# Gate and q projections as seven block products instead of eight, over pairs of token blocks

## The chip, the cores and the metric

The kernel runs on one core of one Trainium2 chip. The metric is device time in microseconds, from one launch. The engines are named as the profile names them: PE (TensorE matmul), PEld (TensorE weight load), DVE (VectorE), ACT (ScalarE), POOL (GpSimd) and SP (SyncE, which here only issues DMAs). Each engine works through its own instruction queue in order and waits on semaphores for the others.

## The reference

One layer of a latent backbone with 2048 latent tokens, 256 context tokens and width 1024, all in float32:

```python
h_lat = _rmsnorm(x, norm_g[i]) * (1.0 + scale) + shift        # (2048, 1024)
h_ctx = _rmsnorm(ctx, norm_g[i]) * (1.0 + scale_c) + shift_c  # (256, 1024)
na_q, na_k, na_v, na_g, r_q, r_k, r_v, r_g = _split_proj(h_lat @ w_in)   # w_in: (1024, 4096)
o_na = _neighbourhood_attention(...)       # 8 heads of 64, 8 x 16 window and all context keys
y_na = _merge(o_na) * silu(na_g)
o_ret = o_f + flip(o_b)                    # 4 retention heads of 128, both directions
y_ret = _head_rmsnorm(o_ret, ret_norm_g) * silu(r_g)
x = x + gate * (concatenate([y_na, y_ret]) @ w_out)
return _rmsnorm(x, final_norm_g)
```

What matters here is the projection h @ w_in, above all the columns of na_q (0 to 511), na_g (1536 to 2047) and r_g (3584 to 4095), which only latent tokens need.

## The kernel before

Activations are kept transposed, 128 rows of the 1024 features to a partition tile (KC = 8 tiles along the feature axis), in four latent blocks of 512 tokens and one context block of 256. Every float32 operand of the projections is split into a rounded high part and the low rest, and a product is made of three matmuls (high x high, high x low, low x high); so each feature tile costs three matmuls. The block `blk[b]` is a pair of tiles, `hhi` and `hlo`, of 16 KB a partition each. Blocks 0 and 1 lie in the pool `hx` and blocks 2 and 3 in the pool `hy`, each with two buffers for each name.

Weights come in sets of 256 columns. `w_raw` loads one in two halves of 512 KB into the pool `st` (four buffers), `w_split` has ACT round the high part `whi` (L336) and POOL subtract it (`wlo`, L338), into the pool `wa` with two buffers of each. `load_w` issues the next set's load on SP's queue.

A unit of work is one of two forms. `tform` (L357) makes 128 columns for 512 tokens: 24 matmuls of 128x512. `tokform` (L368) makes 256 tokens by 256 columns: 48 matmuls of 128x256. Each takes one PSUM bank, of which the pool `pp` has six and the pool `psm` two. Both are generators with eight yields, so that they can be cut into pieces. The tile `o` that a unit's result is written to, on the way to DRAM, has two buffers. `store` puts off the issue of a DMA until the next `tick`; after the k projections the stores go out on ACT's queue.

The order of the work is the order of the program: nothing reorders it within an engine. In time, it is

- the k projections with the preparation of the blocks, by the list `PLAN`;
- `run_jobs`: v for all tokens (`u_v`, whose eviction is two casts on ACT, two subtractions on DVE and eight DMAs, four each on ACT's and SP's queues), four context units, then gates (`u_gate`, one SiLU on ACT) and q (`u_q`, a cast on ACT and a subtraction on DVE), eight units to a set of columns. Beside them `spill_step` writes blocks 2 and 3 to DRAM on SP's queue, and hooks behind the units of three sets prepare the output weights: `wo_gate` (L568, DVE adds one row block of the gate columns, eight times), `wo_row` (L575, four matmuls), `wo_mul` (L579, DVE multiplies a row block of `w_out`; ACT and POOL split it, L583 and L584; ACT stores it), eight times. All of these read one tile `wraw` with a single buffer, reloaded on SP's queue (L565) when the last reader is done;
- attention: 131 steps, in each of which pieces of the remaining projection units (the generator `fill_stream`, 48 units of eight pieces) stand between the matmuls of attention (L754, L781, L783, L802, L804). `quota` hands the pieces out evenly, with `held` = 66 kept for the stage behind. The four last q units come ahead of it, and blocks 2 and 3 are read back during it;
- retention with the output projection.

## Time and profile before

| | us |
|---|---|
| median of 3 runs | 1389.71 (1388.34 to 1392.48) |
| profiled execution, its own time | 1387.86 |
| its span, first to last instruction | 1386.1 |
| PE busy in the span | 1339.7 (97%) |
| DVE / ACT / POOL busy | 641.4 / 530.6 / 494.2 |
| granted TensorE clock, mean | 0.997 |
| v, context, gate and q units (from 166.6 to 561.7) | 395 |
| attention stage (562 to 1037) | 475 |

A line of the chain of waits gives the start, the length and what ran, with the count of instructions that follow each other; the length over the count is their spacing. A line of the instruction groups ends in the busy time and the mean duration of one in ns, and behind the next bar in the idle time of the engine before it and what ended it. A matmul's duration there includes its passage through the array, which overlaps the next one's; the spacing is read from the chain. A line of the order of time gives start, duration, engine, line, operation and in brackets the idle time before it with its releaser. A line of the table of stretches gives the stretch, its length, each engine's busy time with the count of its instructions, the granted clock, the DMA engines' busy share and GB/s.

### The profile page before, as it was taken

Reading aid. Unit: us, or ns where it says so; the run is one execution under the profiler, and the core shown is the slowest. Engines: PE = TensorE matmul, PEld = TensorE weight load, DVE = VectorE, ACT = ScalarE, POOL = GpSimd, SP = SyncE. Lnnn points to the kernel's source line nnn. Section 1 sums busy time; section 2 is a strip of 40 time slices with the busy share of each in tenths; the row PEclk is TensorE's granted clock in tenths of the full one; section 3 lists DMA queues with packets and bytes.
Section 4 is the critical chain, followed back from the end, with each engine's and each line's share of the span. In section 5 each row is a group of like instructions: output and inputs, shape, how many; then the busy total and the mean of one; then the engine's idle time right before and its main releaser. Section 6 shows DMA issues by size and latency. Waiting matters only on the chain.

```text
span 1386.1 us, 22777 instructions
## 1 busy us (share of the span) xinstructions
PE 1339.7 (97%) x8380; PEld 1172.7 (85%) x8380; DVE 641.4 (46%) x1244; ACT 530.6 (38%) x1155; POOL 494.2 (36%) x499
## 2 busy tenths in 40 slices
...
GB/s 315 173 162 125 184 253 279 228 130 106 47 166 131 220 256 258 207 169 208 188 174 211 203 223 267 267 209 161 196 84 261 257 286 287 175 168 168 160 115 129
DMA packets 218705, 270.45 MB, mean 195 GB/s; under 512 B 16865, under 2 KB 163425, under 8 KB 217570
## 3 DMA queue, kind: packets, MB, share of 16 engines
...
## 4 chain that ended last, share of the span: by engine, by line
PE 79%; DVE 7%; DMA 5%; issue 3%; POOL 3%; ACT 2%; SPq 1%; POOLq 0%; ACTq 0%; DVEq 0%
PE mm L357 26%; PE mm L368 19%; PE mm L1198 11%; PE sS L754 4%; PE tr L781 3%; PE po L802 3%; PE mm L921 2%; PE tr L783 2%; PE po L804 2%; PE mm L301 1%; PE mm L1110 1%; PE mm L1109 1%; PE mm L1108 1%; DMA v<-rvS 1%; PE mm L1089 1%
## 5 line engine op out<-in xcount | busy, mean ns | idle before, releaser
L357 PE MATMUL mm<-hhi,whi 128*128 128x512 f32 x640 | 259.0, 405 | 0.0
L357 PE MATMUL mm<-hlo,whi 128*128 128x512 f32 x640 | 253.1, 396 | 5.6 <-DVE hlo L270 2.2
L357 PE MATMUL mm<-hhi,wlo 128*128 128x512 f32 x640 | 252.9, 395 | 0.3 <-DVE wlo L338 0.3
L368 PE MATMUL mm<-whi,hhi 128*128 128x256 f32 x768 | 224.1, 292 | 0.0
L368 PE MATMUL mm<-wlo,hhi 128*128 128x256 f32 x768 | 216.7, 282 | 2.4 <-POOL wlo L338 2.4
L368 PE MATMUL mm<-whi,hlo 128*128 128x256 f32 x768 | 215.5, 281 | 0.0
L338 POOL TENSOR_TENSOR wlo<-st,whi 128x256 fp32r<-128x256 f32 (+1 forms) x97 | 112.3, 1175 | 243.1 <-ACT whi L336 240.6
L785 ACT CAST pt<-tr 128x640 fp32r<-128x640 f32 (+1 forms) x128 | 95.7, 748 | 191.7 <-PE tr L783 181.0
L791 DVE TENSOR_TENSOR pt<-tr,pt 128x640 fp32r<-128x640 f32 (+1 forms) x128 | 113.9, 890 | 91.3 <-ACT pt L785 90.6
L368 PEld LDWEIGHTS mm<-wlo,hhi 128*128 128x128 f32 x768 | 144.6, 188 | 3.1 <-POOL wlo L338 3.0
L357 PEld LDWEIGHTS mm<-hlo,whi 128*128 128x128 f32 x640 | 120.4, 188 | 31.3 <-issue 3.3
L357 PEld LDWEIGHTS mm<-hhi,wlo 128*128 128x128 f32 x640 | 120.1, 188 | 29.4 <-DVE wlo L338 0.7
L368 PEld LDWEIGHTS mm<-whi,hlo 128*128 128x128 f32 x768 | 144.9, 189 | 0.0
L368 PEld LDWEIGHTS mm<-whi,hhi 128*128 128x128 f32 x768 | 144.9, 189 | 0.0
L357 PEld LDWEIGHTS mm<-hhi,whi 128*128 128x128 f32 x640 | 120.3, 188 | 28.5 <-issue 4.6
L774 POOL TENSOR_SCALAR sp<-sp,stt 128x640 f32<-128x640 f32 (+2 forms) x128 | 103.7, 812 | 106.9 <-DVE stt L773 63.0
L763 DVE CUSTOM_DVE_ANT_0 sp<-sS,nb 128x640 f32<-128x640 f32 (+2 forms) x128 | 105.5, 825 | 22.4 <-PE sS L754 13.4
L768 ACT ACTIVATE sp<-sp,stt 128x640 f32<-128x640 f32 (+2 forms) x128 | 107.5, 840 | 15.4 <-DVE stt L763 15.0
L754 PE MATMUL sS<-k,q 128*128 128x256 f32 (+3 forms) x512 | 98.5, 314 | 4.4 <-DVE stt L763 3.4
L1198 PE MATMUL mm<-wor,y 128*128 128x512 f32 x384 | 95.6, 398 | 1.8 <-DVE xt L1207 1.2
L754 PEld LDWEIGHTS sS<-k,q 128*128 128x128 f32 x512 | 83.4, 188 | 11.2 <-DVE stt L763 5.5
L1198 PE MATMUL mm<-won,y 128*128 128x512 f32 x336 | 89.9, 406 | 0.0
...
## 6 DMA issues: line engine op xcount, KB each, us to landing
...
```

Source lines behind the costliest of these rows:

```text
L338: eng.tensor_tensor(l, r, f(h), ALU.subtract)
L357: nc.tensor.matmul(pm[:, :n], ww[:, k, cs], h[:, k, :], start=(k == 0 and i == 0), stop=(k == KC - 1 and i == 2))
L368: nc.tensor.matmul(pm[:, t * WG:(t + 1) * WG], h[:, k, o:o + P], ww[:, k, :], start=(k == 0 and i == 0), stop=(k == KC - 1 and i == 2))
L754: nc.tensor.matmul(o, hd["q"][i][:, hl, j * P:(j + 1) * P], k, start=(hl == 0), stop=(hl == 1))
L763: nc.vector.tensor_tensor_reduce(T["sp"][:, :n], T["s"], nbz[big][:, o:o + n], -1.0, 3e38, ALU.add, ALU.min, T["st"][:, 0:1])
L768: nc.scalar.activation(sp[:, :n], sp[:, :n], AF.Exp, bias=st[:, 0:1], scale=-1.0, accum_out=st[:, 1:2])
L774: nc.gpsimd.tensor_scalar(sp[:, :n], sp[:, :n], st[:, 2:3], 0.0, ALU.mult, ALU.add)
L781: nc.tensor.transpose(tr[:cn, g, :], sp[:, T["lo"] + g * cn:T["lo"] + (g + 1) * cn], ident)
L785: nc.scalar.copy(pt[:, :ng_ + 2, 0, :], tr[:, :ng_ + 2, :])
L791: nc.vector.tensor_tensor(pt[:, :n, 1, :], tr[:, :n, :], f(pt)[:, :n, 0, :], ALU.subtract)
L802: nc.tensor.matmul(po[:, t % 2, :, :], hd["vt"][kr0 // 4 + g][:cn, VORD.index(j), :], pt[:cn, g, :, :], start=(g == 0), stop=False)
L1198: nc.tensor.matmul(pm, yy[:, k, :], ww[:, k, sl], start=(k == 0 and i == 0), stop=(k == 3 and i == 2))
```

## The change

For each set of 256 columns (two column groups of 128) and each pair of token blocks A and B, the product is treated as a 2 by 2 product of blocks: feature halves on the inner side, the two column groups on one outer side and the two token blocks on the other. Eight block products become seven, with sums of weight blocks (`w_sums`) and of token blocks (`h_sums`) ahead and sums of products behind, in the form with 15 additions. `w_set` computes one set: seven `prod` of 12 matmuls each, with the sums of the products taken by DVE out of PSUM and the SiLU, or for q the scale of 0.125 and the split, afterwards (`fin`).

- The pair (0, 1) goes first. Its four token sums, high and low, take the `hy` buffers of blocks 2 and 3; these are spilled first, two parts behind each v unit. Blocks 0 and 1 are spilled during the first pass.
- Between the passes, blocks 2 and 3 are loaded into `hx`, the four context units run, rv (columns 3072) of blocks 2 and 3 runs in four whole units, and the token sums of the pair (2, 3) are made. Then the second pass runs, with its weights loaded again (26 sets are loaded in all, 6 more than before).
- The hooks of the output weights are at the 24 steps of the second pass: `wo_open`, a pause, eight gates, the row, eight muls; four steps to a set, after the second, fourth, sixth and seventh product.
- `fill_stream` now has 44 units, first for blocks 2 and 3 and then for 0 and 1, which are read back during attention. Where the last four q units stood, 24 pieces of it run (`LEAD`).
- The small tiles `rs` and `t0` move from the pool `op` to `st`; `wo_row` uses the pool `psm`.

```diff
+LEAD = 24
...
-    jobs = [(1024, [(u_v, (tp,)) for tp in range(9)]), (1280, [(u_v, (tp,)) for tp in range(9)])]
-    jobs += [(c0, [(u_gate, (ct, b)) for ct in range(2) for b in range(4)]) for c0 in (1536, 1792)]
-    for n, (c0, u) in enumerate(((2560, u_rk), (2816, u_rk), (3072, u_rv), (3328, u_rv))):
-        jobs.insert(2 * n + 1, (c0, [(u, (8,))]))
-    jobs += [(c0, [(u_gate, (ct, b)) for ct in range(2) for b in range(4)]) for c0 in (3584, 3840)]
-    jobs += [(c0, [(u_q, (ct, b)) for b in (2, 3, 0, 1) for ct in range(2)]) for c0 in (0, 256)]
-
-    fseq = [(u_rv, 3072), (u_rk, 2560), (u_rq, 2048), (u_rv, 3328), (u_rk, 2816), (u_rq, 2304)]
+    SETS = (1536, 1792, 3584, 3840, 0, 256)
+    fseq = [(u_rv, 3328), (u_rk, 2560), (u_rq, 2048), (u_rk, 2816), (u_rq, 2304)]
     fseq += [(u_rv, 3328), (u_rv, 3072), (u_rk, 2560), (u_rq, 2048)]
-    wseq = [(c0, 0.125 if us[0][0] is u_q else None) for c0, us in jobs[1:]] + [(c0, None) for _, c0 in fseq]
+    MID = [(2560, u_rk), (2816, u_rk), (3328, u_rv), (3072, u_rv)]
+    wseq = [1280, *SETS, *[c0 for c0, _ in MID], *SETS, fseq[0][1], fseq[1][1]]
...
+    spill = [(b, hl, k) for b in (2, 3, 0, 1) for hl in range(2) for k in range(0, KC, 2)]
...
+    def reload_parts(b):
+        blk[b] = (hx.tile([P, KC, 512], F32R, name="hhi"), hx.tile([P, KC, 512], F32R, name="hlo"))
+        return [(f(blk[b][hl])[:, k:k + 2, :].rearrange("p k t -> p (k t)"), hS[b][hl][:, k * 512:(k + 2) * 512])
+                for k in range(0, KC, 2) for hl in range(2)]
+
+    def h_sums(T, A, B):
+        (ah, al), (bh, bl) = ((f(x) for x in blk[b]) for b in (A, B))
+        tl = {}
+
+        def tile_(key, name, dt=F32R):
+            tl[key] = hy.tile([P, 2, KH, 512], dt, name=name)
+
+        V, G = nc.vector.tensor_tensor, nc.gpsimd.tensor_tensor
+
+        def cut(key, ks, d):
+            t = tl[key]
+            nc.scalar.copy(t[:, 0, ks, :], d)
+            (G if key < 3 else V)(t[:, 1, ks, :], d, f(t)[:, 0, ks, :], ALU.subtract)
+
+        def first(c):
+            if c == 0:
+                tile_(0, "hhi", F32)
+                tile_(3, "hlo")
+            ks, kt = slice(2 * c, 2 * c + 2), slice(KH + 2 * c, KH + 2 * c + 2)
+            d, e = tl[0][:, 0, ks, :], tl[0][:, 1, ks, :]
+            V(d, bh[:, kt, :], bh[:, ks, :], ALU.subtract)
+            G(e, bl[:, kt, :], bl[:, ks, :], ALU.subtract)
+            V(d, d, e, ALU.add)
+            cut(3, ks, d)
+
+        def second(c):
+            if c == 0:
+                tile_(2, "hhi")
+            ks = slice(2 * c, 2 * c + 2)
+            d = tl[0][:, 0, ks, :]
+            V(d, d, ah[:, ks, :], ALU.add)
+            V(d, d, al[:, ks, :], ALU.add)
+            cut(2, ks, d)
+
+        def third(c):
+            if c == 0:
+                tile_(4, "hlo")
+            ks, kt = slice(2 * c, 2 * c + 2), slice(KH + 2 * c, KH + 2 * c + 2)
+            d = tl[0][:, 0, ks, :]
+            V(d, ah[:, kt, :], d, ALU.subtract)
+            V(d, d, al[:, kt, :], ALU.add)
+            cut(4, ks, d)
+
+        def fourth(k):
+            if k == 0:
+                tile_(1, "hhi")
+                T.extend(tl[n] for n in (1, 3, 2, 4))
+            o = env["st"].tile([P, 2, 512], F32, name="o3", bufs=1)
+            d, e = o[:, 0, :], o[:, 1, :]
+            V(d, bh[:, k, :], ah[:, k, :], ALU.subtract)
+            G(e, bl[:, k, :], al[:, k, :], ALU.subtract)
+            V(d, d, e, ALU.add)
+            cut(1, k, d)
+
+        return [lambda fn=fn, c=c: fn(c) for fn, n in ((first, 2), (second, 2), (third, 2), (fourth, KH)) for c in range(n)]
+
+    def w_sums(rw):
+        cut2 = lambda t: t.rearrange("p k w -> p (k w)").rearrange("p (s h k c) -> p s h k c", s=2, h=2, k=KH)
+        a11, a21 = rw[0][:, :, 0:P], rw[0][:, :, P:WG]
+        a12, a22 = rw[1][:, :, 0:P], rw[1][:, :, P:WG]
+        W, tl = {}, {}
+
+        def cut(key, n, s, r):
+            if n not in tl:
+                tl[n] = cut2(wa.tile([P, KC, WG], F32R, name=("whi", "wlo")[n % 2]))
+            t = W[key] = tl[n][:, s]
+            nc.scalar.copy(t[:, 0], r)
+            nc.gpsimd.tensor_tensor(t[:, 1], r, f(t)[:, 0], ALU.subtract)
+
+        def p0():
+            cut("a11", 0, 0, a11)
+            cut("a12", 0, 1, a12)
+
+        def p1():
+            cut("a22", 1, 0, a22)
+            nc.vector.tensor_tensor(a22, a21, a22, ALU.add)
+            nc.vector.tensor_tensor(a21, a11, a21, ALU.subtract)
+            nc.vector.tensor_tensor(a11, a22, a11, ALU.subtract)
+            nc.vector.tensor_tensor(a12, a12, a11, ALU.subtract)
+            cut("s2", 1, 1, a11)
+
+        def p2():
+            cut("s1", 2, 0, a22)
+            cut("s3", 2, 1, a21)
+
+        def p3():
+            cut("s4", 3, 0, a12)
+            load_w()
+
+        return W, [p0, p1, p2, p3]
+
+    def plain_next(res):
+        def p1():
+            res.append(w_split(wcur.pop(0)))
+
+        return [None, p1, None, load_w]
+
+    def w_set(c0, W, T, A, B, ahead, hooks):
+        isq = c0 < 512
+        t1, t3, t2, t4 = (tuple(t[:, e] for e in range(2)) for t in T)
+        b11, b21 = (tuple(x[:, e * KH:(e + 1) * KH, :] for x in blk[A]) for e in range(2))
+        b22 = tuple(x[:, KH:, :] for x in blk[B])
+        lay = (lambda x: x.rearrange("p (j r c) -> p j r c", r=8, j=4)) if isq else (lambda x: x)
+        pv_ = (lambda x: x.rearrange("p (r j c) -> p j r c", r=8, j=4)) if isq else (lambda x: x)
+
+        def prod(w, h):
+            pm = ptile()
+            for k in range(KH):
+                for i, (ww, hh) in enumerate(((w[:, 0], h[0]), (w[:, 0], h[1]), (w[:, 1], h[0]))):
+                    nc.tensor.matmul(pm, ww[:, k, :], hh[:, k, :], start=(k == 0 and i == 0), stop=(k == KH - 1 and i == 2))
+            return pv_(pm)
+
+        def out_tile(extra=False):
+            o = env["st"].tile([P, 2, 512], F32R, name="o3", bufs=1) if extra else op.tile([P, 2, 512], F32R, name="o")
+            return o, [lay(f(o)[:, e, :]) for e in range(2)]
+
+        def fin(o, ct, b):
+            if isq:
+                nc.scalar.activation(o[:, 0, :], f(o)[:, 1, :], AF.Copy, scale=0.125)
+                nc.vector.scalar_tensor_tensor(o[:, 1, :], f(o)[:, 1, :], 0.125, f(o)[:, 0, :], ALU.mult, ALU.subtract)
+                store(qS[c0 // P + ct][b], f(o))
+                return
+            g = f(o)[:, 1, :]
+            nc.scalar.activation(g, g, AF.Silu)
+            dst = gS[(c0 - 1536) // P + ct] if c0 < 2048 else ggS[(c0 - 3584) // P + ct]
+            store(dst[:, b * 512:(b + 1) * 512], g)
+
+        def step(n):
+            tick()
+            if ahead[n]:
+                ahead[n]()
+            if hooks:
+                h = hooks.pop(0)
+                if h:
+                    h()
+
+        V = nc.vector.tensor_tensor
+        (oa, (_, xa)), (ob, (yb, xb)) = out_tile(), out_tile(True)
+        nc.scalar.copy(yb, prod(W["a11"], b11))
+        V(xa, prod(W["a12"], b21), yb, ALU.add)
+        step(0)
+        m4 = prod(W["a22"], t4)
+        fin(oa, 0, A)
+        V(xb, prod(W["s2"], t2), yb, ALU.add)
+        step(1)
+        m5 = prod(W["s1"], t1)
+        V(yb, prod(W["s3"], t3), xb, ALU.add)
+        oc, (_, xc) = out_tile()
+        V(xc, m4, yb, ALU.add)
+        od, (_, xd) = out_tile()
+        V(xd, m5, yb, ALU.add)
+        V(xb, m5, xb, ALU.add)
+        fin(oc, 1, A)
+        step(2)
+        m3 = prod(W["s4"], b22)
+        fin(od, 1, B)
+        V(xb, m3, xb, ALU.add)
+        fin(ob, 0, B)
+        step(3)
...
-    hooks = {8: [wo_open] + [g(k) for k in range(7)], 9: [g(7), wo_row] + [m(k) for k in range(6)], 10: [m(6), m(7)]}
-    qu, w_next = run_jobs(jobs, wr[3], hooks)
+    def unit(g, nsp=0):
+        for _ in g:
+            pass
+        tick()
+        for _ in range(nsp):
+            spill_step()
+
+    def strassen(T, A, B, W, hook, last):
+        for n, c0 in enumerate(SETS):
+            if n + 1 < len(SETS):
+                Wn, ahead = w_sums(wcur.pop(0))
+            else:
+                Wn, ahead = last, plain_next(last)
+            w_set(c0, W, T, A, B, ahead, hook)
+            W = Wn
+
+    load_w()
+    w0, w1 = wr[3], w_split(wcur.pop(0))
+    load_w()
+    for b in (2, 3):
+        for w, c0 in ((w0, 1024), (w1, 1280)):
+            for tp in (2 * b, 2 * b + 1):
+                unit(u_v(w, c0, tp), 2)
+    for w, c0 in ((w0, 1024), (w1, 1280)):
+        unit(u_v(w, c0, 8))
+    T = []
+    hs = h_sums(T, 0, 1)
+    W, ahead = w_sums(wcur.pop(0))
+    for n, (w, c0, tp) in enumerate([(w, c0, tp) for w, c0 in ((w0, 1024), (w1, 1280)) for tp in range(4)]):
+        for _ in u_v(w, c0, tp):
+            if hs and n:
+                hs.pop(0)()
+        tick()
+        if n == 4:
+            ahead[0]()
+        if n == 5:
+            ahead[1]()
+    while hs:
+        hs.pop(0)()
+    ahead[2]()
+    ahead[3]()
+    mid = []
+    strassen(T, 0, 1, W, [spill_step] * 24, mid)
+    while spill:
+        spill_step()
+    for d in reload_parts(2):
+        nc.sync.dma_start(*d)
+    (wk0,) = mid
+    wk1 = w_split(wcur.pop(0))
+    load_w()
+    for d in reload_parts(3):
+        nc.sync.dma_start(*d)
+    unit(u_rk(wk0, 2560, 8))
+    wk2 = w_split(wcur.pop(0))
+    unit(u_rk(wk1, 2816, 8))
+    wk3 = w_split(wcur.pop(0))
+    load_w()
+    load_w()
+    unit(u_rv(wk2, 3328, 8))
+    unit(u_rv(wk3, 3072, 8))
+    T = []
+    hs = h_sums(T, 2, 3)
+    W, ahead = w_sums(wcur.pop(0))
+    ahead[0]()
+    for n in range(4):
+        for _ in u_rv(wk3, 3072, 4 + n):
+            if hs:
+                hs.pop(0)()
+        tick()
+        if n == 0:
+            ahead[1]()
+    while hs:
+        hs.pop(0)()
+    ahead[2]()
+    ahead[3]()
+    wo_steps = [wo_open, None] + [g(k) for k in range(8)] + [wo_row] + [m(k) for k in range(8)]
+    last = []
+    strassen(T, 2, 3, W, wo_steps, last)
+    w_next = last + [w_split(wcur.pop(0))]
+    flush()
 
     left.close()
     psx.close()
     sx.close()
     env.update(pp=psm, st=pool(sx, "st2", 2, side="right"))
+    wseq += [c0 for _, c0 in fseq[2:]]
...
-        order = [(kind, *a_) for kind, c0 in fseq[:4] for b in range(2) for a_ in units(kind, b)]
-        order += [(kind, *a_) for b in range(4) for kind, c0 in fseq[4:6] for a_ in units(kind, b)]
-        order += [(kind, *a_) for kind, c0 in fseq[6:] for b in (2, 3) for a_ in units(kind, b)]
+        order = [(kind, *a_) for kind, c0 in fseq[:3] for b in (2, 3) for a_ in units(kind, b)]
+        order += [(kind, *a_) for b in (2, 3, 0, 1) for kind, c0 in fseq[3:5] for a_ in units(kind, b)]
+        order += [(kind, *a_) for kind, c0 in fseq[5:] for b in (0, 1) for a_ in units(kind, b)]
...
-    env["fill"] = fill_stream(w_next)
-    NF = 48 * 8
+
+    env["fill"] = fill_stream(*w_next)
+    NF = 44 * 8
...
-        run(n)
+        fill(LEAD // 4)
+        tick()
...
-        quota = (NF - held) * (t + 1) // (NT + 3) - done
+        quota = (NF - held - LEAD) * (t + 1) // (NT + 3) - done
```

124 lines of the change are left out of this document (40 added, 84 removed).

## The prediction

> **What bounds the kernel now.** I read the page's engine table first, then the chain of waits in order of time from 150 to 570 us, and the table of stretches.
>
> ```profile
> PE 1339.7 (97%) x8380; PEld 1172.7 (85%) x8380; DVE 641.4 (46%) x1244; ACT 530.6 (38%) x1155; POOL 494.2 (36%) x499
> ...
> 279.96 44.79 PE mm L357 x192
> 324.75 5.68 PE mm L368 x48
> ...
> 380.86 55.95 PE mm L357 x240
> 436.81 1.72 PE mm L575 x4
> 438.53 123.21 PE mm L357 x528
> ...
> 8.00:34.00 26.00, 22.59 (x74) 8.11 (x75) 17.39 (x30) 12.94 (x19) 14.05 (x11) 1.00 1.09 344
> 438.00:562.00 124.00, 124.00 (x534) 99.61 (x533) 24.14 (x26) 26.02 (x44) 26.27 (x23) 1.00 0.68 225
> 562.00:1037.00 475.00, 465.80 (x3531) 442.88 (x3531) 324.45 (x724) 260.62 (x545) 218.78 (x247) 1.00 0.71 198
> ```
>
> TensorE sets the time: from 280 to 562 us the chain is matmuls end to end, with no wait in it. Its rows give the prices. One 128x512 matmul takes 44.79/192 = 0.233 us (the 0.40 of the groups is latency), so a Strassen product of 12 takes 2.80, a set of seven 19.6; the four plain units of the same columns and pair take 4 x 5.60 = 22.4. A token-form unit of 48 matmuls takes 5.68. The attention stage (562 to 1037) has PE busy 465.8 of 475 us too.
>
> **The saving.** Gate and q now take 6 column sets x 8 units x 24 = 1152 matmuls; after, 6 x 2 pairs x 84 = 1008. 144 x 0.233 = **-33.6 us** of TensorE. It appears in two places: ahead of attention four rv units and the three units' worth of LEAD come in and the plain gate and q go out (7 x 5.68 + 12 x 19.6 - 48 x 5.60 = +6.2), and the filler inside attention falls from (384-66)/131 = 2.43 to (352-66-24)/131 = 2.00 pieces a step: 56 x 0.71 (5.68/8) = -39.8. The chain of waits inside attention:
>
> ```profile
> 708.08 0.58 PE sS L754 x4
> 708.66 0.71 PE mm L368 x6
> 709.38 0.44 PE tr L781 x4
> 710.03 0.71 PE mm L368 x6
> 710.74 0.48 PE po L802 x4
> 711.46 0.70 PE sS L754 x4
> ```
>
> This is a step of attention with two pieces: 3.38 us, TensorE without a gap (the rest of the tr and po pieces is among those the view leaves out). DVE, the next busiest, needs 324.45/131 = 2.48 a step. So I count the attention saving in full; the bound is 0 to +10, as much again as the 9.2 us that TensorE idles there now.
>
> **What is added beside TensorE.** The groups of instructions by form:
>
> ```profile
> L579 DVE TENSOR_TENSOR wraw<-wraw,gacc 128x1024 f32<-128x1024 f32 x8 | 9.8, 1226 | 60.6 <-DMA wraw<-in_w_out_dram 52.7 <-ACT gacc L576 7.9
> L338 POOL TENSOR_TENSOR wlo<-st,whi 128x1024 fp32r<-128x1024 f32 x25 | 60.2, 2434 | 204.1 <-ACT whi L336 204.1
> L336 ACT CAST whi<-st 128x1024 fp32r<-128x1024 f32 x26 | 26.0, 1047 | 4.8 <-DVE o L425 1.9 <-DVE o L387 1.1 <-ACT o L461 0.9
> L584 POOL TENSOR_TENSOR g<-wraw,g 128x512 fp32r<-128x512 f32 x16 | 20.4, 1294 | 105.2 <-ACT g L583 105.2
> L583 ACT CAST g<-wraw 128x512 fp32r<-128x512 f32 x16 | 9.2, 619 | 48.4 <-DVE wraw L579 47.5 <-DMA woS<-g 0.6 <-ACT o L393 0.4
> L1207 DVE TENSOR_TENSOR xt<-mm,xt 128x512 f32<-128x512 f32 x64 | 43.8, 687 | 85.9 <-PE mm L1198 85.9
> ```
>
> In a steady set of 19.6 us the weight sums and evictions take POOL 7 x 1.29 = 9.1, ACT 12 x 0.62 = 7.4, DVE 11 x 0.69 = 7.6 (15 in a q set, 10.4): under half a set each, each weight cut about four products ahead. I price them at nothing, with the seven products as cover (uncovered, up to 9 us a set). The 16 further spills and 6 further weight loads also lie beside products; in the v stage they bring 2 x 0.52 MB a unit, whose cover is six PSUM banks, 6 x 5.68 = 34 us. The moved tiles rs and t0 cost nothing: same instructions, other buffers. Three places are not steady.
>
> **First: the token sums of blocks 0 and 1.** The sums are one chain in program order. A "first" part is POOL 2.43, DVE 1.23, ACT 1.05, DVE 1.23 = 5.9; the next two-slice part adds DVE 2.46 + ACT 1.05 + DVE 1.23; with the other parts' overlaps the "third" ends at about 26 us; each of the four "fourth" parts waits for its single buffer: POOL 1.29 + DVE 0.69 + ACT 0.62 + POOL 1.29 = 3.9. Sum about 41 us; ACT is through eight parts at 32 and through all at 40. They are issued inside v units 1 and 2, so those units' evictions queue behind them on ACT and DVE, and units 3 to 7 behind these. One such eviction in ACT's order of time:
>
> ```profile
> 170.91 0.38 ACT L424 CAST o<-mm 128x256 fp32r<-128x256 f32 x1 [4.90 <-PE mm L368]
> 171.78 0.37 ACT L424 CAST o<-mm 128x256 fp32r<-128x256 f32 x1 [0.49 <-DVE o L425]
> 172.64 2.04 ACTq L434 DMA_DIRECT2D vB<-o  x4
> ```
>
> The eviction is 1.73 us on ACT (it waits for DVE's halves) and its four stores 2.04: 3.75. Unit 4 is through at 40 + 3 x 3.75 = 51, and only behind it stand the cuts of a11 (ACT 0.62, POOL 1.29): 53. TensorE is through unit 7 at 7 x 5.68 - 1 = 39: 14 us late. s1's cut stands behind unit 7 and the four DVE sums: about 71, due at 50: 21 late. If the stores cost ACT nothing, both are about 9 late. I take **+17** (9 to 21), nearer the rows as they stand.
>
> **Second: between the passes.** Call the last product's end E. Block 3 needs block 1's buffers, free at E, and in SP's queue it stands behind one weight set, block 2 and another weight set; the first starts about E-2.5, when the plain split of 2560 frees its buffer. 2 x 1.05 + 2 x 4.19 = 10.5 MB, at the 344 GB/s of 8 to 34 us, is 30.5 us: block 3 lands at E+28, the set for a11 (1.05 MB behind it) at E+31. Its cut stands on ACT ahead of the sums, so the sums start in effect at E+28.6. On TensorE 8 units and four products need no token sums past the first ready ones: m5 is due at E + 45.4 + 11.2 = E+56.6. It needs the last sum and a free bank; rv unit 4's eviction stands behind eight parts, the a22 and s2 cuts hold the rest by about 5 us, s1's cut follows: 48 us after the start, E+77. **+20**. Bounds: no queueing, 42 us from E+26, +11; loads at the 269 GB/s of a row quoted below for the clock, 9 us later, +30.
>
> **Third: the gate and w_out rows,** in the second pass. Their rows in DVE's order of time, where it waits for the one wraw buffer:
>
> ```profile
> 403.03 1.28 DVE L568 SCALAR_TENSOR_TENSOR gacc<-wraw,silc,gacc 128x1024 f32<-128x1024 f32 x1 [3.84 <-DMA wraw<-in_w_ada_dram]
> 408.23 1.28 DVE L568 SCALAR_TENSOR_TENSOR gacc<-wraw,silc,gacc 128x1024 f32<-128x1024 f32 x1 [3.92 <-DMA wraw<-in_w_ada_dram]
> ...
> 452.54 1.22 DVE L579 TENSOR_TENSOR wraw<-wraw,gacc 128x1024 f32<-128x1024 f32 x1 [12.13 <-DMA wraw<-in_w_out_dram]
> 461.79 1.23 DVE L579 TENSOR_TENSOR wraw<-wraw,gacc 128x1024 f32<-128x1024 f32 x1 [8.02 <-DMA wraw<-in_w_out_dram]
> ...
> 489.32 1.23 DVE L579 TENSOR_TENSOR wraw<-wraw,gacc 128x1024 f32<-128x1024 f32 x1 [7.94 <-DMA wraw<-in_w_out_dram]
> ```
>
> A mul comes every (489.32-452.54)/4 = 9.2 us: multiply, cast, two POOL differences, reload. Before, nothing of the gate units waited on DVE, and six banks at 5.6 us covered ACT's lag. After, a step averages 4.9 us, and five to seven DVE evictions of a set stand behind these waits. From mul 0 to mul 7 DVE needs 7 x 9.2 = 64.4 us, TensorE 13 x 2.80 = 36.4 (sets numbered from 0: mul 0 stands at the end of set 2, mul 7 behind the sixth product of set 4). Behind the last mul come its casts and differences, four stores, s4's cut and the copy that frees a11's bank, about 7.5 us, then the last product, 2.8; from its place eight products were due (22.4). 64.4 + 1.2 + 10.3 - 36.4 - 22.4 = 17.1. The weights of the first filler unit stand behind this on ACT and POOL: +3.9. The gates (5.2 us apart, weight loads ahead of some in SP's queue) make the row matmul, itself unchanged at 1.72, wait: +2. **+23**; bounds: 12 (TensorE waits only for the freed bank) and 32 (a cycle of 10.4, the last in the trace).
>
> **The clock after a wait** I price from the table of stretches:
>
> ```profile
> 1104.00:1108.00 4.00, 2.10 (x13) 1.91 (x14) 3.81 (x9) 1.39 (x2) 1.27 (x1) 0.91 0.94 269
> 1108.00:1112.00 4.00, 3.46 (x14) 2.66 (x13) 2.15 (x8) 1.34 (x2) 1.14 (x1) 0.50 0.89 280
> 1112.00:1116.00 4.00, 3.82 (x13) 3.09 (x14) 0.78 (x3) 2.10 (x6) 2.19 (x4) 0.74 1.06 378
> ```
>
> Behind a wait near 1106 the granted clock is 0.50 and 0.74 in two stretches of 4 us: 2.0 + 1.0 = 3 us lost where TensorE is the limit. One such: **+3** (0 to 9 for three).
>
> **Sum:** -33.6 + 17 + 20 + 23 + 3 = +29.4 on the profiled execution's own 1387.9 us (span 1386.1, 1.8 around it): 1417.3; the median of the runs, 1389.7, lies 1.8 above that execution: **1419 us**. All low bounds give -2, all high +58 (+68 with attention's).
>
> **Rivals.** (a) Faster: the token sums stay hidden. They do from a chain of about 24 us downwards, for then v's evictions fit the banks' 34 us and m5's sum comes by E+57; then -33.6 + 23 + 3 = -7.6, 1382. For it: DVE and POOL are under half busy; against: 1226 ns for 1024 elements is what the trace shows, and the order is serial. (b) The w_out rows also hide, through banks I undercount: -33.6, 1356; against it the 9.2 us. (c) All three at their low ends: 1388 less 2 and plus 1.8: 1388, no change. (d) The waits cool the clock in the mul phase: every step of 9.2 us holds 5.6 of products and a gap of 3.6; at half clock the products take 11.2, 2 us over the cycle, seven times, plus 3 us at each of the other waits: +20, 1439. For it the 0.50 row; against it, that it followed one gap among denser work. The Trainium skill (TensorE: Matmul & The Clock Gate, Part 1) states this as a rule: about 3.4 us of idle drops the array to half rate, and as long of work raises it; the row agrees, and by the rule alone (d) would be likelier than I make it. (e) Attention becomes bound by its dependencies with two pieces a step: +10 on the forecast, 1429; the step above speaks against.
>
> **Chances.** Forecast 0.61 (its own range 1398 to 1440), (a) 0.15, (b) 0.04, (c) 0.04, (d) 0.12, (e) 0.04. Less than 0.3% (4 us) can't be told from no change. Faster 0.19, same 0.04, slower 0.77. The range 1371 to 1440 holds the forecast, (a), (c), (e) and half of (d).
>
> **What would show it.** Right: TensorE waits of over 10 us at the first set's a11 or s1, at the second pass's first s1 product, and in sets 4 and 5 of that pass with DVE waiting for wraw; v evictions in a lump some 40 us behind their units; attention near 436 us. Wrong: fewer than 20 us of TensorE waits between v and attention, a mul cycle under 6 us, or sums done in 24.

## The result, and the profile after

The changed kernel takes 1488.14 us (median; 1483.65 to 1495.31) against 1389.03 for the kernel before on the same chip: a ratio of 1.072 (95% interval 1.067 to 1.076), 99 us slower. The forecast was 1419 (1371 to 1440), slower with a chance of 0.77: the sign is right, the loss was put at 29 us and is more than three times that. The profiled execution took 1483.65 us, its span is 1481.8.

From the page, the engine table and the row of the granted clock:

```profile
PE 1335.8 (90%) x8236; PEld 1165.8 (79%) x8236; DVE 787.6 (53%) x1420; ACT 590.4 (40%) x1245; POOL 628.7 (42%) x585
...
PEclk9999999699999598888999999999999999999999
```

TensorE issues 144 matmuls fewer, as intended, and is busy for only 4 us less; it now idles for 146 us of the span (46 before). No other engine is near its limit: DVE, the next, is at 53%. The clock row shows where it happens: of its slices of 37 us the eighth (259 to 296 us) stands at 0.6, the fourteenth (482 to 519) at 0.5 and the sixteenth to nineteenth (556 to 704) at 0.8; before, all forty were at 0.9 or more.

By stages, against the kernel before (spans 1481.8 and 1386.1):

| from the start of v | before | after | difference | forecast |
|---|---|---|---|---|
| v, context, gate, q, up to the first attention matmul | 395.0 | 536.3 | +141.3 | +69 |
| attention, first to last sS matmul | 465.1 | 427.3 | -37.8 | -39.8 |
| ahead of v, and behind attention | 526.0 | 518.2 | -7.8 | 0 |

The gain came as forecast. The whole miss is in the first row: 6.2 us of it is work that moved, 135 us are stalls, where 63 were expected. The table of stretches divides it (start:end, width, then busy time and count of each engine, the granted clock, the DMA engines' share and GB/s): v and the first token sums, the first pass, the part between the passes with the second pass's first products, the rest of the second pass, the 24 pieces ahead of attention, and attention.

```profile
163.00:291.00 128.00, 106.69 (x867) 105.91 (x865) 42.31 (x56) 22.92 (x46) 31.46 (x16) 0.93 0.59 187
291.00:417.00 126.00, 121.88 (x509) 97.77 (x510) 50.17 (x77) 43.74 (x78) 58.85 (x44) 0.97 0.58 197
417.00:526.00 109.00, 74.83 (x466) 67.72 (x465) 39.79 (x38) 27.23 (x38) 50.21 (x29) 0.83 0.45 165
526.00:669.00 143.00, 110.47 (x426) 85.41 (x425) 62.11 (x76) 45.03 (x77) 67.78 (x49) 0.88 0.60 197
669.00:700.00 31.00, 18.61 (x148) 17.99 (x147) 6.81 (x7) 6.90 (x10) 9.84 (x9) 0.88 0.66 178
700.00:1127.00 427.00, 420.01 (x3122) 396.99 (x3121) 318.11 (x712) 248.27 (x513) 205.38 (x228) 1.00 0.77 213
```

The idle time of TensorE ahead of attention is 21.3 + 4.1 + 34.2 + 32.5 + 12.4 = 104.5 us. The other 30 are in the busy columns: 426 matmuls of 128x512 are 99 us at the spacing of 0.233 us that steady products have, and took 110.47; counted in the same way for each stretch (0.118 us for a 128x256), the excess is 4 + 3 + 10 + 11 + 1 = 29 us. Some 5 us of that is the last matmul ahead of each wait, counted with its whole passage of 0.40 us; about 25 us are products at a lower clock behind waits, and the granted clock of 0.83 to 0.93 stands beside them.

The waits of TensorE from 150 to 720 us (engine, line and tile that waited, what released it; us in total, times, longest):

```profile
PE mm L622 <- ACT wlo L579: 19.5, 1, 19.5
PE mm L622 <- ACT whi L579: 15.1, 2, 11.9
PE mm L622 <- ACT o L651: 10.7, 2, 7.8
PE sS L952 <- DMA q<-qS: 10.6, 1, 10.6
PE mm L695 <- DVE gacc L688: 10.2, 1, 10.2
PE mm L365 <- DVE o L406: 7.8, 1, 7.8
PE mm L622 <- ACT o L442: 7.7, 1, 7.7
PE mm L365 <- POOL wlo L338: 7.5, 6, 2.0
PE mm L622 <- ACT g L703: 6.5, 3, 5.1
```

L622 is the Strassen product. It waits 11.9 us for the first pass's a11 and 19.5 for the second pass's a22 (cuts on ACT that stand behind token sums and evictions), and 7.8 and 5.1 in the sets with the w_out rows, where the releasers are an eviction and a row's cast on ACT. The row matmul (L695) waits 10.2 for the gates' sum. L365, the token-form units, waits 7.8 for a v bank, and L622 7.7 for a bank that an rv eviction (L442) holds. The first attention matmul waits 10.6 for its queries, a stall that the prediction doesn't have. The rows of the instructions around these waits, in order of time (start, duration, engine, line, operation, count, idle time before it and its releaser; SPq is SP's issue queue):

```profile
246.70 5.86 POOL L525 TENSOR_TENSOR hhi<-hhi 128x1024 fp32r<-128x1024 f32 x2 [53.19 <-ACT hhi L524]
252.51 2.28 POOL L563 TENSOR_TENSOR o<-hlo 128x512 f32<-128x512 f32 x1
...
250.22 3.41 DVE L552 TENSOR_TENSOR hhi<-hhi 128x1024 f32<-128x1024 f32 x1 [2.30 <-POOL hhi L525]
253.67 2.20 DVE L553 TENSOR_TENSOR hhi<-hhi,hlo 128x1024 f32<-128x1024 f32 x1
...
288.43 2.07 ACTq L415 DMA_DIRECT2D vB<-o  x4
290.54 1.14 ACT L579 CAST whi<-st 128x512 fp32r<-128x512 f32 x2 [2.60 <-DMA vB<-o]
...
448.25 1.23 DVE L533 TENSOR_TENSOR hhi<-hhi 128x1024 f32<-128x1024 f32 x1 [26.52 <-DMA hhi<-hS]
459.96 3.40 DVE L535 TENSOR_TENSOR hhi<-hhi 128x1024 f32<-128x1024 f32 x1 [10.49 <-POOL hhi L534]
...
454.19 0.62 ACT L579 CAST whi<-st 128x512 fp32r<-128x512 f32 x1 [3.05 <-DMA st<-in_w_in_dram]
455.57 0.62 ACT L579 CAST whi<-st 128x512 fp32r<-128x512 f32 x1 [0.77 <-DMA st<-in_w_in_dram]
...
454.88 2.68 POOL L580 TENSOR_TENSOR whi<-st,whi 128x512 fp32r<-128x512 f32 x2 [9.27 <-ACT whi L579]
457.52 4.76 POOL L534 TENSOR_TENSOR hhi<-hlo 128x1024 f32<-128x1024 f32 x2
...
612.12 1.22 DVE L699 TENSOR_TENSOR wraw<-wraw,gacc 128x1024 f32<-128x1024 f32 x1 [6.16 <-DMA wraw<-in_w_out_dram]
622.02 1.23 DVE L699 TENSOR_TENSOR wraw<-wraw,gacc 128x1024 f32<-128x1024 f32 x1 [8.07 <-DMA wraw<-in_w_out_dram]
631.01 1.23 DVE L699 TENSOR_TENSOR wraw<-wraw,gacc 128x1024 f32<-128x1024 f32 x1 [5.39 <-DMA wraw<-in_w_out_dram]
...
650.71 33.93 SPq L176 DMA_DIRECT2D st<-in_w_in_dram  x4
684.74 1.31 SPq L915 DMA_DIRECT2D k<-kS  x2
686.74 1.14 SPq L924 DMA_DIRECT2D q<-qS  x2
```

Five things are to be seen. A sum on DVE takes 1.22 us alone, 3.41 and 2.20 where POOL runs beside it. The first pass's cut of a11 and a12 (290.54) stands on ACT behind a v eviction and the issue of its stores. The second pass's first sum was ready to start at 448.25, but the next step on DVE came at 459.96: it waited for POOL's first difference, which stood behind the cut of a11 and a12 (454.88), and that cut waited for its raw weights, which landed at 454.2 and 455.6. The muls follow each other at 9 to 12 us (three of the eight are shown), with DVE waiting for the row. And SP stands at a weight load from 650.71 to 684.64, because its buffer is not free, before it may issue the keys and queries of attention.

### The profile page after: what moved, and what is told of

It is laid out like the page before. It is cut to its first block, busy times and chain, and to the rows that moved or that the text cites. A ratio compares the mean times of both kernels' runs of the same rounds, so it can differ in the third digit from the quotient of the medians.

```text
span 1481.8 us, 23106 instructions
## 1 busy us (share of the span) xinstructions
PE 1335.8 (90%) x8236; PEld 1165.8 (79%) x8236; DVE 787.6 (53%) x1420; ACT 590.4 (40%) x1245; POOL 628.7 (42%) x585
## 3 DMA queue, kind: packets, MB, share of 16 engines
q1 hardware_dynamic: 192674, 227.30, 51.4%
## 4 chain that ended last, share of the span: by engine, by line
PE 42%; issue 4%; DVE 4%; DMA 4%; POOL 3%; ACT 2%; SPq 1%; ACTq 0%; POOLq 0%; DVEq 0%
PE mm L1391 10%; PE mm L365 8%; PE sS L952 5%; PE mm L354 4%; PE tr L979 3%; PE po L1000 3%; PE mm L1114 2%; PE tr L981 2%; PE po L1002 2%; DMA v<-rvS 1%; PE mm L1303 1%; PE mm L1302 1%; PE mm L1301 1%; POOL g L704 1%; PE mm L1282 1%
## 5 line engine op out<-in xcount | busy, mean ns | idle before, releaser
L365 PE MATMUL mm<-whi,hhi 128*128 128x256 f32 x768 | 225.4, 293 | 7.8 <-DVE o L406 7.8
L365 PE MATMUL mm<-wlo,hhi 128*128 128x256 f32 x768 | 218.6, 285 | 3.6 <-POOL wlo L338 3.6
L365 PE MATMUL mm<-whi,hlo 128*128 128x256 f32 x768 | 217.8, 284 | 0.0
L983 ACT CAST pt<-tr 128x640 fp32r<-128x640 f32 (+1 forms) x128 | 95.7, 748 | 153.9 <-PE tr L981 152.5
L365 PEld LDWEIGHTS mm<-whi,hhi 128*128 128x128 f32 x768 | 147.5, 192 | 8.0 <-issue 8.0
L365 PEld LDWEIGHTS mm<-wlo,hhi 128*128 128x128 f32 x768 | 146.9, 191 | 4.5 <-POOL wlo L338 4.5
L365 PEld LDWEIGHTS mm<-whi,hlo 128*128 128x128 f32 x768 | 147.8, 192 | 0.0
L961 DVE CUSTOM_DVE_ANT_0 sp<-sS,nb 128x640 f32<-128x640 f32 (+2 forms) x128 | 105.4, 824 | 31.1 <-DMA nb<-in_rpb_t_dram 24.0
L622 PE MATMUL mm<-hhi,whi 128*128 128x512 f32 x336 | 101.4, 407 | 17.9 <-ACT whi L579 15.1
L338 POOL TENSOR_TENSOR wlo<-st,whi 128x256 fp32r<-128x256 f32 (+1 forms) x75 | 86.2, 1165 | 68.3 <-ACT whi L336 62.4
L952 PE MATMUL sS<-k,q 128*128 128x256 f32 (+3 forms) x512 | 100.4, 318 | 14.0 <-DMA q<-qS 10.6
L354 PE MATMUL mm<-hhi,whi 128*128 128x512 f32 x256 | 107.3, 419 | 0.0
L354 PE MATMUL mm<-hlo,whi 128*128 128x512 f32 x256 | 101.0, 394 | 5.5 <-DVE hlo L271 2.3
L354 PE MATMUL mm<-hhi,wlo 128*128 128x512 f32 x256 | 101.2, 395 | 0.0
L952 PEld LDWEIGHTS sS<-k,q 128*128 128x128 f32 x512 | 82.7, 189 | 21.0 <-issue 10.7
L580 POOL TENSOR_TENSOR whi<-st,whi 128x512 fp32r<-128x512 f32 x48 | 63.3, 1340 | 76.6 <-ACT whi L579 75.1
L622 PEld LDWEIGHTS mm<-hhi,whi 128*128 128x128 f32 x336 | 65.7, 196 | 35.0 <-ACT whi L579 15.7
L622 PE MATMUL mm<-hhi,wlo 128*128 128x512 f32 x240 | 73.9, 424 | 18.3 <-ACT o L651 10.7
```

Of the source, the lines that this page charges most:

```text
L338: eng.tensor_tensor(l, r, f(h), ALU.subtract)
L354: nc.tensor.matmul(pm[:, :n], ww[:, k, cs], h[:, k, :], start=(k == 0 and i == 0), stop=(k == KC - 1 and i == 2))
L365: nc.tensor.matmul(pm[:, t * WG:(t + 1) * WG], h[:, k, o:o + P], ww[:, k, :], start=(k == 0 and i == 0), stop=(k == KC - 1 and i == 2))
L580: nc.gpsimd.tensor_tensor(t[:, 1], r, f(t)[:, 0], ALU.subtract)
L622: nc.tensor.matmul(pm, ww[:, k, :], hh[:, k, :], start=(k == 0 and i == 0), stop=(k == KH - 1 and i == 2))
L952: nc.tensor.matmul(o, hd["q"][i][:, hl, j * P:(j + 1) * P], k, start=(hl == 0), stop=(hl == 1))
```

## The experiments

The first table sets all kernels side by side. A set runs from its first product to that of the next; a steady one takes 19.45. "Between" is from the last product of the first pass to the first of the second. In brackets stand the values without any wait; from e10 on (e11 and e12 excepted) the four context units, 22.7 us, stand ahead of the first pass instead of between the passes.

| kernel | us | a11 of pass 1 starts (265.5; 288.2) | sets of pass 1 | between (45.4; 22.7) | sets of pass 2 | last product to attention (17.0) |
|---|---|---|---|---|---|---|
| after | 1488.1 | 291.2 | 27.8, then 19.5 | 56.8 | 52.5 19.7 33.4 19.4 32.2 38.6 | 30.3 |
| e1_rows_once | 1462.1 | 293.6 | 27.8, then 19.5 | 56.5 | 50.6 19.7 22.0 19.4 23.4 33.8 | 29.0 |
| e2_spread | 1480.2 | 277.4 | 37.4, then 19.5 | 56.7 | 50.8 19.5 34.4 19.5 30.7 39.5 | 28.8 |
| e3_no_reload | 1478.4 | 290.2 | 28.9, then 19.5 | 51.2 | 49.4 19.5 35.1 19.7 31.1 39.9 | 30.3 |
| e4_dve_sums | 1471.9 | 290.4 | 27.8, then 19.5 | 56.3 | 42.7 19.7 35.0 19.5 30.7 38.4 | 29.9 |
| e5_rows | 1466.5 | 291.7 | 28.1, then 19.5 | 56.7 | 53.1 19.6 30.4 19.7 19.4 24.7 | 42.1 |
| e6_mid | 1446.4 | 287.7 | 28.1, then 19.5 | 55.8 | 25.0 19.5 32.5 19.7 32.3 37.8 | 27.1 |
| e7_first | 1455.2 | 271.5 | 34.0, then 19.5 | 58.1 | 33.6 19.5 33.3 19.7 32.1 39.1 | 29.4 |
| e8_order | 1477.9 | 292.3 | 28.0, then 19.5 | 57.1 | 50.5 19.7 34.9 19.4 30.8 39.6 | 20.0 |
| e9_all | 1421.6 | 269.3 | 40.2, then 19.5 | 51.8 | 30.5 19.4 21.1 19.5 24.2 29.2 | 35.6 |
| e10_moved | 1439.8 | 309.9 | 19.5 (21.2 at the row) | 48.7 | 19.5 20.4 26.5 19.7 26.3 27.2 | 32.5 |
| e11_fit | 1426.0 | 270.2 | 32.7, then 19.5 | 64.8 | 29.6 19.5 21.1 20.0 22.4 27.9 | 29.5 |
| e12_qfirst | 1414.5 | 267.2 | 33.5 19.6 22.7 19.7 19.4 19.5 | 51.4 | 21.1 22.7 26.0 24.5 22.5 26.1 | 29.4 |
| e13_two | 1415.1 | 315.5 | 19.5 (21.2 at the row) | 29.0 | 30.3 19.5 23.8 19.8 20.6 21.5 | 24.5 |
| e14_one | 1414.0 | 314.8 | 19.5 (21.2 at the row) | 28.9 | 30.4 19.4 26.4 20.0 19.4 20.5 | 23.6 |
| e15_late | 1395.7 | 298.9 | 21.6 21.2 24.8 19.5 21.2 19.5 | 31.3 | 27.3 20.9 27.6 19.5 19.5 19.5 | 17.2 |
| e16_turn | 1394.5 | 302.6 | 23.8 19.4 19.4 19.7 21.2 19.5 | 28.3 | 31.1 19.4 25.7 19.4 20.8 21.1 | 19.4 |
| e17_qlast | 1403.4 | 299.8 | 19.5 (21.2 at the row) | 32.9 | 36.1 19.5 19.8 19.5 20.5 24.0 | 25.2 |

e12, e15, e16 and e17 ran several times beside the kernel before and have an interval; each of the others ran once, beside a kernel before of 1385 to 1391 us on the same chip. The changed kernel's four executions lie 12 us apart, and its stages are those of the execution of 1483.65 us; so a difference of a few us between total times says little, and the stages are what is read. Differences below are to the median, 1488.1; to the profiled execution they are 4.5 us less. The cuts of code of e1 to e9 are against the changed kernel, those of e10 and e11 against e9, of e12 against e11, of e13 and e15 against e14, of e16 against e15 and of e17 against e16; `...` marks what is left out. (e10 also moves 22.7 us of units from attention to the part between: without waits its value there is 45.4.)

### Four single changes: which cause holds which stall

The theory was the prediction's: the reload of the row holds the second pass's sets, the sum chain with its order the first, block 3's landing the start of the second. Against it stood the engines' own work, and POOL beside DVE.

**(e1_rows_once) The row tile loaded once** (rows of the gate and output weights after the first load of each are left out).

```diff
     def wo_gate(k):
-        wo_load(a["w_ada"][(k + 1) * P:(k + 2) * P, 2 * D:] if k + 1 < KC else a["w_out"][0:P, :])
...
-        if k + 1 < KC:
-            wo_load(a["w_out"][(k + 1) * P:(k + 2) * P, :])
```

> The changed kernel with the single row tile loaded once only: the 8 gate steps and the 8 row multiplies keep their place and their work, but the 15 later loads of the tile are left out (so the scaled w_out rows have other values). Theory W, DVE waits for the reload of that tile and the sets behind it stand: sets 2, 4 and 5 of the second pass, 33.2, 31.7 and 38.7 us in the changed kernel, come back to 19.5 to 24, the multiplies start 5 to 6 us apart instead of 10.4, the time is 1440 to 1458 us. Rival: the evictions and sums of a set are too slow on DVE and POOL by themselves when row work is mixed in; then sets 4 and 5 stay above 28 us and the time is above 1470.

1462.1, 26 us less, of which sets 2, 4 and 5 of the second pass give 25 (33.4 + 32.2 + 38.6 against 22.0 + 23.4 + 33.8). So the reloads are about half of their 46 us, 11 of it in set 2, where the row matmul no longer waits for the gates. The time lies between the two forecasts. DVE's rows, in order of time, show something of the other half:

```profile
593.13 1.23 DVE L698 TENSOR_TENSOR wraw<-wraw,gacc 128x1024 f32<-128x1024 f32 x1 [1.18 <-POOL g L703]
599.76 1.23 DVE L698 TENSOR_TENSOR wraw<-wraw,gacc 128x1024 f32<-128x1024 f32 x1 [4.81 <-POOL g L703]
```

With the data always there, a mul still waits 4.81 us for POOL's difference of the mul before, in POOL's queue between the weight cuts. Neither theory is the whole: about half is the load, and the rest is left with every row at hand; that it is all the order of the queues is argued from rows like these, not shown.

**(e2_spread) The token sums spread**, one part to five steps of v.

```diff
-        for _ in u_v(w, c0, tp):
-            if hs and n:
+        for i, _ in enumerate(u_v(w, c0, tp)):
+            if hs and (8 * n + i) % 5 == 2:
```

> The changed kernel with the ten parts of the first sums set out one per 5 steps over the eight v units of blocks 0 and 1, instead of one per step from the second unit on. Theory S, the sums are late because they are lumped ahead of the v evictions: the a11 product, 25.7 us late in the changed kernel, is at most 10 late, the first set takes under 23 us instead of 27.8, time 1455 to 1468. Rival D, the v stage's transfers and the length of the chain itself (46.8 us for eight units of 5.68) set the end: the a11 product stays 18 or more late and the time is above 1475.

a11 starts 13.8 us earlier, still 11.9 late, and set 0 takes 9.6 more; neither forecast has that. TensorE's rows in order of time:

```profile
291.56 5.09 PE L622 MATMUL mm<-hlo,wlo 128*128 128x512 f32 x12 [6.09 <-ACT wlo L579]
...
303.92 5.69 PE L622 MATMUL mm<-hhi,whi 128*128 128x512 f32 x12 [4.21 <-ACT whi L579]
```

The wait went to the next weight cuts, and behind each the 12 matmuls take 5 to 6 us, where 12 spacings are 2.8: the clock. Spreading the sums moved the wait and hardly shortened it.

**(e3_no_reload) No reload** (the second pass computes from blocks 0 and 1; blocks 2 and 3 are left out of it).

```diff
-    for d in reload_parts(2):
-        nc.sync.dma_start(*d)
+    blk[2], blk[3] = blk[0], blk[1]
...
-    for d in reload_parts(3):
-        nc.sync.dma_start(*d)
```

> The changed kernel with the 16 transfers that bring blocks 2 and 3 back left out between the passes: the second pass, and what follows, reads blocks 0 and 1 once more (8.4 MB less is read, the output is of other values). Theory L, the second sums begin late because block 3 lands at 32 us behind the end of the first pass: the chain then starts some 35 us earlier, set 0 of the second pass takes under 24 us instead of 52.7, the eight units between the passes 46 to 52 instead of 56.9, time 1440 to 1452. Rival C, the chain of 55 us over three engines is too long in any case: it ends 15 or more us behind the units also when it starts at once, and the time is above 1460.

Only 10 us less, where 1440 to 1452 was the theory. With every block at hand the first sum starts 5 us behind the last product (416.5), and then (DVE and POOL in order of time):

```profile
421.56 1.22 DVE L533 TENSOR_TENSOR hhi<-hhi 128x1024 f32<-128x1024 f32 x1
451.81 3.41 DVE L535 TENSOR_TENSOR hhi<-hhi 128x1024 f32<-128x1024 f32 x1 [29.03 <-POOL hhi L534]
...
434.94 4.75 POOL L338 TENSOR_TENSOR wlo<-st,whi 128x1024 fp32r<-128x1024 f32 x2 [2.29 <-ACT whi L336]
446.87 2.56 POOL L580 TENSOR_TENSOR whi<-st,whi 128x512 fp32r<-128x512 f32 x2 [7.18 <-ACT whi L579]
449.38 4.75 POOL L534 TENSOR_TENSOR hhi<-hlo 128x1024 f32<-128x1024 f32 x2
```

DVE waits 29 us for POOL's first difference (L534), which is free of data waits but stands in POOL's queue behind the cut of a11 and a12 (L580); that cut waits for weights which come through two raw buffers one set after the other. Here the weights alone set the start of the sums, 35 us behind the last product; in the changed kernel it was 43, so the reload's own part is some 8 us. The rival's chain, too long in any case, was not tested, since it didn't start at once.

**(e4_dve_sums) All sums on DVE.**

```diff
-        V, G = nc.vector.tensor_tensor, nc.gpsimd.tensor_tensor
+        V = G = nc.vector.tensor_tensor
```

> The changed kernel with every sum of token blocks on DVE, none on POOL (the weights' sums as they were). Theory P, DVE and POOL slow each other: without POOL beside it DVE's 128x1024 sums take 1.1 to 1.3 us each (3.4 and 2.2 beside POOL), the first chain goes from 46.8 to at most 38 us and the second from 55.4 to at most 45, and the time falls by 10 to 25, to 1459 to 1474. Rival: the two engines work side by side and DVE then carries the 12 moved operations of both passes' sums alone, 10 to 20 us more on the chain; the time is 1484 to 1510.

16 us less, 10 of them in set 0 of the second pass: the sums no longer pass through POOL's queue. DVE in order of time:

```profile
254.06 1.22 DVE L552 TENSOR_TENSOR hhi<-hhi 128x1024 f32<-128x1024 f32 x1
255.32 1.23 DVE L553 TENSOR_TENSOR hhi<-hhi,hlo 128x1024 f32<-128x1024 f32 x1
```

The two operations that took 3.41 and 2.20 are back at 1.22. But the chains are hardly shorter: the first (233 to 278) takes 45.6 us for 46.8 and the second 54.9 for 55.4, where at most 38 and 45 were expected, since DVE now does POOL's share too. The time came as forecast, the way to it didn't: the second chain starts 10.7 us earlier.

### Four orders

Each takes one stall by order; e6 and e7 move sums to DVE besides. **(e5_rows) The rows earlier and further apart**, their stores on SP:

```diff
-                defer(1, lambda hl=hl, sl=sl, w=w: nc.scalar.dma_start(woS[hl][k, :, sl], f(w)[:, hl, :]))
+                nc.sync.dma_start(woS[hl][k, :, sl], f(w)[:, hl, :])
...
-    wo_steps = [wo_open, None] + [g(k) for k in range(8)] + [wo_row] + [m(k) for k in range(8)]
+    wo_steps = [g(k) for k in range(8)] + [None, wo_row] + [f for k in range(7) for f in (m(k), None)][:13] + [m(7)]
```

> The changed kernel with all row work kept, but its tile opened among the four rv units between the passes, the gate steps in the first eight steps of the second pass, the row matmul two steps behind the last of them, and the row multiplies at every second step (one per 9.7 us of products in place of one per 4.86), the scaled rows stored from SP at once in place of from ACT a step later. Theory W2: a set stands because the multiplies are asked for twice as fast as their cycle (10.4 us in the changed kernel, 6.6 with the reloads left out) and the engines' queues are in order; at half the rate sets 2 to 5 of the second pass take 19.5 to 23 us each (33.2, 19.4, 31.7 and 38.7 in the changed kernel), the time is 1438 to 1450. Rival: the multiply's own operations and the evictions collide at any rate; sets with multiplies stay above 25 us, time above 1462.

22 us less, where 38 to 50 was the theory: sets 2, 4 and 5 fall to 30.4, 19.4 and 24.7, and 12 us are lost again ahead of attention (42.1 for 30.3), since the muls, 10 to 14 us apart, now end there. The time is in the rival's range.

**(e6_mid) Between the passes:** block 2 reloaded inside the last set, the pair taken as (3, 2), so that the sums which need block 2 alone come first, all sums on DVE, low halves one part late, cuts behind the first unit of rv (`early` issues the rest of the spills and then block 2's loads).

```diff
+    strassen(T, 0, 1, W, [spill_step] * 20 + [early], mid)
...
+    hs = h_sums(T, 3, 2)
     unit(u_rk(wk0, 2560, 8))
     wk2 = w_split(wcur.pop(0))
+    hs.pop(0)()
...
-    strassen(T, 2, 3, W, wo_steps, last)
+    strassen(T, 3, 2, W, wo_steps, last)
```

> The changed kernel with the time between the passes put in another order and nothing left out: block 2's reload is issued in the last set of the first pass (behind the last read of block 0) in place of behind its last weight load, the second pass takes block 3 as its first and block 2 as its second block, so that the first sums need block 2 alone, the sums are all on DVE with the low half of a part one part later, they are spread over the eight units, and the weights of the first set are cut behind the fifth unit and behind the first three sums rather than ahead of all sums. Theory O (order): sums and weights are ready when the units end: the first sum starts within 8 us of the end of the first pass (32 in the changed kernel), units 46 to 50 us and set 0 of the second pass 19.5 to 26 (56.9 and 52.7), time 1438 to 1455. Rival B: transfers, weight cuts and eight sums parts are too much for 45 us in any order; set 0 stays above 35 us, time above 1460.

Set 0 falls from 52.5 to 25.0 us, the largest gain of one order (42 us in all). The units between keep their 10 us (55.8, where the theory had 46 to 50). Since the order and the move of the sums to DVE came together, their shares stay open.

**(e7_first) The first sums:** on DVE, low halves late, spread from the first unit, the cuts behind unit 3.

```diff
-            if hs and n:
+            if hs and (8 * n + i) % 6 == 2:
...
-        if n == 4:
+        if n == 3:
             ahead[0]()
-        if n == 5:
             ahead[1]()
```

> The changed kernel with the first sums all on DVE, the low half of a part one part later, one part per 6 steps from the first of the eight v units on, and the weights of the first set cut behind the fourth of them (a11, a12, a22 and the weight sums, when the first v weights' tiles come free). The second sums get the DVE and the later low half too, in their old order. Theory O: the a11 product is at most 8 us late (25.7 in the changed kernel, 11.9 with spreading alone) and set 0 of the first pass takes at most 23 us (27.8; 37.4 with spreading alone); the chain after the first pass shortens by 5 to 12 as well; time 1445 to 1460. Rival D: the v units' own transfers keep the evictions late; a11 stays 15 or more late or set 0 above 30; time above 1466.

a11 at 271.5, 6 us from its value without waits, but set 0 takes 34.0: 13.5 us of the 34 are won here. The first pass's set was to be 23 us at most; at 34 it is where the rival put it. The rest of the 33 us is the second pass, where the sums on DVE, with the low halves late, take set 0 to 33.6 (42.7 with the sums on DVE alone, e4).

**(e8_order) SP's queue:** the weight load that waits for a buffer goes behind the first head's loads.

```diff
     wseq += [c0 for _, c0 in fseq[2:]]
-    load_w()
...
     load_v(heads[0], (0, 1, 2))
+    load_w()
```

> The changed kernel with one weight load of SP (whose tile comes free only when POOL has cut the last weights) moved from ahead of the first head's loads to behind them. Theory: q then lands 8 to 11 us earlier against the last product, attention starts at once behind the 24 units ahead of it: 1472 to 1478. Rival: the first head's q waits for something else as well (its store, or space), and the wait stays: 1482 to 1486.

SP in order of time:

```profile
650.69 11.71 SPq L176 DMA_DIRECT2D st<-in_w_in_dram  x2
662.50 1.18 SPq L914 DMA_DIRECT2D k<-kS  x2
...
664.35 1.11 SPq L923 DMA_DIRECT2D q<-qS  x2
```

1477.9, as the theory had it. The queries are issued at 664 instead of 687, and the way to attention takes 20.0 instead of 30.3: 10.3 us, the whole of the wait for q.

### Put together, and what it runs into

**(e9_all) All four, the row tile two deep, cuts between the passes on DVE.**

```diff
+        t = wo["p"].tile([P, D], F32R, name="wraw", bufs=2)
...
-    wk2 = w_split(wcur.pop(0))
+    wk2 = w_split(wcur.pop(0), 0)
...
-        return [None, p1, None, load_w]
+        return [None, p1, p1, load_w]
```

> All the orders of the four runs before in one kernel, nothing left out: first sums spread (one part per 5 steps) and on DVE, the time between the passes re-ordered, the row work over the second pass at every second step, SP's weight load behind the first head's loads; and three more: both of the weights that follow a pass are cut within its last set, two of the cuts between the passes are on DVE, and the row tile is two deep (its low half written in place), so that a reload is under way while the row before is worked on. Theory: the stages' stalls are separate and their gains add up: about 12 + 30 + 35 + 8 us off 1484, 1390 to 1405, and in the best case, all four gone, the 1370 that the 33.6 us of removed matmuls would give. Rival: the engines are short in sum, and what one stage gives another takes; above 1425.

1421.6, between the two forecasts: 67 of the 99 us are back. What is left is above all set 0 of both passes (20.8 and 11 us), the rows (16) and the way to attention (18.6).

**(e10_moved) Units moved as cover:** the context units ahead of the first pass, four rv units from attention to the part between, the gates in the first pass.

```diff
+    unit(u_rk(wk[0], 2560, 8))
+    next_w()
+    unit(u_rk(wk[1], 2816, 8))
...
+        steps[2 * k + 1] = lambda k=k: (spill_step(), wo_gate(k))
...
-    strassen(T, 3, 2, W, wo_steps, last)
+    strassen(T, 3, 2, W, [m(k // 3) if k % 3 == 0 else None for k in range(24)], last)
...
-    NF = 44 * 8
+    NF = 40 * 8
```

> Nothing left out, the work between v and attention dealt out otherwise: the four k and rv units of the context block are moved from between the passes to ahead of the first pass (22.7 us more between the first sums and the first product that needs them, and the space of the row work free from there on), four rv units of columns 3328 for blocks 2 and 3 are moved from attention to between the passes in their place, both blocks' reloads are issued ahead of the weight loads, the gate steps run in the first pass, the row multiplies at every third step of the second (14.6 us apart), sums on DVE, SP's order at attention's start as in the run before last. Theory: all four stalls were ones of order, each step now has its inputs early: set 0 of both passes under 22 us, no set of the second pass over 21, attention starts within 3 us of its 24 units, 1355 to 1380. Rival: in-order queues keep set 0 of the first pass above 30 us or the sets with multiplies above 24; then 1395 or more, no better than the kernel before.

Set 0 of both passes is at 19.5, but only in the second pass is the stall gone. In the first it moved ahead of a11, which starts at 309.9, 21.7 us late (in e9, 3.8 and 20.8 in set 0): TensorE now waits at a context unit (until 288.4), for the cut of its weights. The longest wait of e10 ahead of attention (255 to 660 us):

```profile
PE mm L365 <- ACT whi L336: 13.4, 1, 13.4
```

And at 1439.8 it takes 18 us more than e9. The source view of attention's first matmul (count, ns, first and last start), of this kernel and then of the changed one:

```profile
L972 PE MATMUL sS<-k,q x512: 274/291/564, 649.0 to 1079.1; 128*128 128x256 f32 x86, 128*128 128x384 f32 x44, 128*128 128x512 f32 x21, 128*128 128x288 f32 x20
```

```profile
L952 PE MATMUL sS<-k,q x512: 277/291/579, 699.5 to 1126.8; 128*128 128x256 f32 x86, 128*128 128x384 f32 x44, 128*128 128x512 f32 x21, 128*128 128x288 f32 x20
```

Attention takes 430.1 us instead of 427.3, with 22.7 us of TensorE work less in it: below two pieces a step it isn't bound by TensorE any more, which idles for 21 us there instead of 7, and its wait for DVE's stt tile goes from 3.4 to 12.9 us. Work taken out of it there is work added elsewhere.

**(e11_fit, e12_qfirst) Both reloads ahead of the weight loads, spills spread, row stores on SP; then the q sets first.** The second also undoes the early reload of block 3 and puts the row stores back on ACT.

```diff
-    strassen(T, 0, 1, W, [spill_step] * 20 + [early], mid)
+    strassen(T, 0, 1, W, [spill_step] * 20 + [early, None, early3], mid)
```

> Nothing left out. As the run with all four orders in one (1421.6 us), with the context units again between the passes, and these differences: both blocks' reloads are issued ahead of the weight loads that follow the first pass; block 3's eight stores to the side are one per unit instead of two; a22's cut and the weight sums come two v units later; the row tile is one deep as in the changed kernel, gates begin between the passes, the row matmul stands three steps behind the last gate, the multiplies every second step, the reload of the row ahead of the stores, all of them from SP. Theory: each set turns round on one output tile (first eviction of a set waits for the landing of the last store of the set before), so what ACT and DVE do in front of that store lengthens the set one for one; with the stores off ACT's queue the sets with multiplies take 19.5 to 22 us (21.1, 19.4, 24.3, 29.1 before), set 0 of the second pass under 24 (30.6), attention starts within 25 us of the last product (35.9): 1385 to 1400. Rival: the row's own work on DVE, POOL and ACT is what lengthens the sets, wherever its stores are issued: sets with multiplies stay at 24 to 30 and the time above 1410.

```diff
-    SETS = (1536, 1792, 3584, 3840, 0, 256)
+    SETS = (0, 256, 1536, 1792, 3584, 3840)
```

> Nothing left out. The best stages of the runs before in one kernel (first sums as in the last run, with the a22 cut one v unit and the s1 cut two units earlier; between the passes as in the run of 1421.6, with the first sum ahead of the first unit and the weight sums one unit later; rows as in the last run, their stores again on ACT's queue a step later), and the two q column sets first in each pass, the four gate sets last, so that the row multiplies fall into the sets whose outputs need only a Silu on ACT. Theory: 1426 less 12 (time between the passes), less 7 (s1's late cut there), less 5 to 10 (sets with multiplies at 19.5 to 22 us instead of 21 to 28, q stored long before attention): 1395 to 1405. Rival: gate sets lengthen as much as q sets did, 1412 or more. Either way it then stands against the kernel before by 3 rounds.

The first came out at 1426.0, a time in the rival's range: the part between takes 64.8 us, since the weights that the units there need now stand behind 8 MB of blocks. The second gives 1414.5, the rival's time too, ratio 1.0184 (1.0135 to 1.0232), with set 0 of the second pass at 21.1 but every set behind it 3 to 7 us long.

**(e13_two, e14_one) Context units ahead, half-row muls; the turn-round tile two deep or one.** The tile o3 carries each set's running sum and has one buffer; the question was whether its turn makes the sets long.

```diff
-            o = env["st"].tile([P, 2, 512], F32R, name="o3", bufs=1) if extra else op.tile([P, 2, 512], F32R, name="o")
+            if extra:
+                turn.append(0)
+            o = (env["st"] if len(turn) % 2 else wo["p"]).tile([P, 2, 512], F32R, name="o3", bufs=1) if extra else op.tile([P, 2, 512], F32R, name="o")
```

> Nothing left out. The four k and rv units of the context block stand ahead of the first pass (so the row tiles' space is free from there on and the first sums have 22.7 us more), four rv units alone between the passes; gates in the first pass, 16 half-row multiplies over the second (two of each three steps), stores from SP; and the output tile on which consecutive sets turn round two deep (a second one of 4 KB in the row space, where the tile of scaled halves is one deep instead). Theory T (turn-round): with two the sets with multiplies take 19.5 to 20.5 us, the first pass and its set 0 too; between the passes 12 to 20 us are lost since only 22.7 us of units cover the sums; 1375 to 1395. Rival: the sets with multiplies stay above 22 us since the engines' work itself is in the way; 1400 or more.

> As the other kernel of this pair, with the turn-round tile one deep as in the changed kernel (and the tile of scaled halves two deep). Theory T: sets with multiplies take 22 to 25 us, the time is 12 to 25 us above the other's. Rival: within 5 us of it.

1415.1 and 1414.0: no difference, as the rival said, so nothing shows that these sets wait for the tile's turn (the two kernels differ in the tile of scaled halves as well, which could hide something). Both start a11 27 us late. ACT and SP of the first, in order of time:

```profile
290.22 0.37 ACT L405 CAST o<-mm 128x256 fp32r<-128x256 f32 x1 [9.87 <-DMA vB<-o]
...
283.88 14.04 SPq L415 DMA_DIRECT2D vB<-o  x16
```

SP issues 16 stores of v behind a weight load, the result tile comes free late, ACT waits 9.87 us for it, and the cut behind that eviction keeps TensorE waiting 12.3 us, a stall of the same kind as e10's.

**(e15_late) Cuts ahead of evictions:** the weights of the context units are cut before the last v evictions, each eviction one unit late, the cuts of s1, s3 and s4 before the last sums; the bias of attention is made before v (`mm` runs a unit's matmuls alone).

```diff
-    for g in late:
-        unit(g)
-    unit(u_rk(wk[0], 2560, 8))
+    late.append(mm(u_rk(wk[0], 2560, 8)))
+    unit(late.pop(0))
     next_w()
+    hs.pop(0)()
...
+    for ct in range(3):
+        bias(0, 0, ct)
```

> As the one-deep kernel of the last pair, nothing left out, with the engines' queues given in this order ahead of the first pass: each context unit's weights are cut as soon as the matmuls that used their tile are given, and the last three v evictions and the context evictions come behind those cuts; the last two sums parts stand behind the cuts as well; between the passes the cuts of s1, s3 and s4 come ahead of the last four sums parts; the first row is multiplied at the end of the first pass and the last one four steps ahead of attention; at attention's start the bias is loaded ahead of v. Theory Q (queue order): the a11 product of the first pass starts 24 to 28 us late of the ideal no more but at most 8, at 290 to 297 us instead of 315; set 0 of the second pass falls from 30 to 22 to 27, attention starts 3 to 6 us earlier against the last product: 1414 less 20 to 30, 1384 to 1394, level with the kernel before. Rival: the v evictions themselves (ACT and DVE in turns, two output tiles, 4 us each) are the limit; a11 stays above 305 us and the time above 1402.

1395.65, ratio 1.0060 (1.0038 to 1.0083). That is just above the 1384 to 1394 of the theory, and far from the rival. a11 starts 16 us earlier, and the 24 pieces go over into attention without a wait (17.2 for 17.0). Of the sets of the first pass, 1 and 2 take 21.2 and 24.8, and here ACT does wait for the single tile:

```profile
361.44 0.58 ACT L659 COPY o<-mm 128x512 f32<-128x512 f32 x1 [4.38 <-DMA qS<-o]
```

**(e16_turn, e17_qlast) That tile two deep again, block 3's reload ahead of the row stores; and the same with the q sets last.**

```diff
-    steps[18], steps[22] = wo_row, lambda: back(3)
+    steps[18], steps[21] = wo_row, lambda: back(3)
```

> As the last run (1395.65 us), with the turn-round tile two deep (the tile of scaled halves one deep) and block 3's reload issued ahead of the stores of the first scaled row instead of behind them. Theory T2: the first eviction of a set no longer waits for the landing of q's store; sets 1 and 2 of the first pass fall from 21.2 and 24.8 to 19.5 to 20.5, set 2 of the second from 27.6 to at most 24; block 3 lands 5 us earlier and the first four units and set 0 of the second pass take 3 to 6 us less; 1375 to 1387, below the kernel before. Rival: as in the pair before, the tile makes no difference and the sets stay as they are: 1391 to 1397.

```diff
-    SETS = (0, 256, 1536, 1792, 3584, 3840)
+    SETS = (1536, 1792, 3584, 3840, 0, 256)
```

> As the other run of this pair, with the four gate column sets first and the two q sets last in each pass, as in the changed kernel. Theory T2: with two turn-round tiles the order of the sets does not matter, within 4 us of the other. Rival R: the row work, which then also falls into a q set, and q's late stores cost again what they cost in the first re-ordered runs: 6 to 15 us above the other.

1394.5, ratio 1.0042 (1.0027 to 1.0057), and 1403.4, 1.0098 (1.0081 to 1.0116). The second buffer does what was said of it (sets 1 and 2 at 19.4), yet the time is the rival's and can't be told from that of the kernel ahead of it, the intervals overlap: a11 starts 4 us later, and set 0 of the second pass takes 4 more where 3 to 6 less was expected. With the q sets last the time is 9 us worse, as rival R said, so their place counts: set 0 of the second pass and the part between are 5 us longer each and the way to attention 6, against 6 us less in set 2 of the second pass and 4 in set 0 of the first.

TensorE's waits in the fastest of them (150 to 640 us), and the stretch of its second pass's start:

```profile
PE mm L365 <- POOL wlo L338: 6.3, 6, 1.9
PE mm L630 <- ACT hhi L524: 5.6, 4, 2.0
PE mm L630 <- DVE o L669: 3.7, 2, 2.3
```

```profile
426.00:485.00 59.00, 49.60 (x275) 41.51 (x275) 47.00 (x46) 19.73 (x30) 17.48 (x12) 0.88 0.50 179
```

The waits that the view lists, of which these are the longest, are 28 us together, where the changed kernel has 104; products now wait for cuts of token sums (`hhi`, L524) and their evictions by 2 us at a time. In the stretch DVE is busy 47 of 59 us, which suggests that there the sums themselves set the time and not their place in a queue; no run tests it.

## Why the prediction was wrong, and where it was right

**The saving: right.** 144 matmuls fewer; attention gained 37.8 us of the 39.8 expected, and the steady sets take 19.45 us with no gap, so that weight sums, cuts, evictions and spills do lie beside the products. (The weight loads added are 5 sets, not 6: 58 halves are loaded instead of 48.) Rival (e), attention bound by its dependencies, falls for two pieces a step; e10 shows that it is true just below.

**The first token sums: +17, measured 34** (a11 25.7 late, set 0 8.4 long). The mechanism is the one given, evictions lumped behind the sums and cuts behind these; the size was off. a11 came 57.8 us after the start of the chain of sums (233.4) where 53 was said: the chain took 46.8 us instead of 41, 29.5 instead of 26 for its first six parts (3.2 of that in the two DVE rows beside POOL above, which the step priced at their duration alone) and 4.3 instead of 3.9 for each of the last four. And TensorE's v units, without waits, end 32.1 us after the chain's start, where the account, starting all engines together, put 39: the evictions ahead already ran late, and the chain began 7 us later in TensorE's schedule. Together that is 12 of the 17 us missed; most of the rest comes of taking 17 where the account's own step to s1 gave 21.

**Between the passes: +20, measured 45** (the units 11.4 long, set 0 33.0). The step that failed is "block 3 lands at E+28 ... so the sums start in effect at E+28.6". With E = 416.5, block 3 landed at E+31.7, but the sums went on only at E+43 (459.96). POOL's first difference started at E+41.0 behind the cut of a11 and a12, whose raw weights landed at E+38 and E+39 where E+31 was said. The prediction put that cut on ACT's queue ahead of the sums and didn't follow it into POOL's. e3 shows the step wrong: without any reload the same wait stands, 29 us long. This late start is 12 of the 24 us by which the s1 product (517.4) missed E+77. The other 12 lie between the start and that product, 60 us where 48 was said: the chain took 55.4. TensorE's long waits there stood at a22 (19.5) and s2 (7.7), not at s1.

**The w_out rows: +23, measured 46.** The wait for the single tile is there, the muls 10.4 us apart on the mean where 9.2 was said, which is 9 us over the seven, and the row matmul waited 10.2 where 2 was said. e1 shows that the loads make half of the loss; the way of each mul through POOL and ACT between cuts and evictions is the likely other half. "Before, nothing of the gate units waited on DVE" was the right question with too short a list of what waits. Rival (b) falls.

**The start of attention: not in the sum, 10.6.** The prediction moved loads past SP's queue without naming who issues next behind one that waits for a buffer; e8 gives it back whole.

**The clock: +3, measured about 25.** Rival (d) described the mechanism, at +20 in the mul phase; it works behind every wait of the second pass and of the first sums. The number of waits was the term that was mis-sized, "one such". The row quoted for the price (0.50 and 0.74 behind a wait) was itself a fair one: 12 matmuls in 5 to 6 us behind a wait are some 3 us lost. But the row agrees with the rule that the prediction puts beside it only in the half rate: the longest wait there is 1.18 us, and TensorE was idle for 1.9 of the 4 us, so there waits far shorter than the rule's were enough.

**Rival (a),** the sums hidden at 1382, falls with the chain of 47 us where it needed 24; (c) with it. The named sums make 34 + 45 + 46 + 10.6 = 136 us, the clock within them, beside 6.2 of moved work and 37.8 less in attention; the rest up to the 95.7 between the spans, -8, is ahead of v (3.4) and behind attention (4.4) and wasn't followed up.

**Can it be had?** The best order found takes back 94 of the 99 us and stays 0.4% above the kernel before. Without any stall the change would stand at 1389 - 34 = 1355 us, so some 40 are still lost there (1355 is an estimate from the saving alone), by the table above all at the first a11 (14, of which 3 are a later start of v), in set 0 of the two passes (16), in set 2 of the second pass (6) and between the passes (6). Whether another order or another split of the sums over DVE and POOL wins those is open; it wasn't tried.
